# Score products of 64-channel heads on all 128 rows: the lo parts of the keys stored on both halves of the partitions

## The chip, the cores and the metric

The kernel runs on one core of a Trainium2 chip. Its time is the device time of one execution, in microseconds (us); given are the median, the lowest and the highest of three runs. TensorE (PE) computes matrix products, VectorE (DVE) and ScalarE (ACT) elementwise work, GpSimd (POOL) a little of both, and SyncE (SP) issues the transfers.

## What is computed

A network of four layers on 512 tokens of 1024 channels: two hybrid layers (retention, pooling, neighbourhood attention, attention to a memory of 256 tokens, a gated sum of the four, and a feed-forward block), one layer of sliding-window attention beside latent attention, and one layer of dilated attention; the last two are each followed by attention to a memory and by a feed-forward block. What the change touches is the score product of every attention whose heads have 64 channels, here in the words of the reference:

```
scores = jnp.einsum('bhncd,bhnmd->bhncm', qc, kc) * d_intra          # retention
sc = jnp.einsum('bhrnqd,bhrnwkd->bhrnqwk', qg, kg) * (d ** -0.5) + bias   # neighbourhood
sc = jnp.einsum('bhsd,bhmd->bhsm', q, mk) * (q.shape[-1] ** -0.5)    # memory, hybrid layers
s = jnp.einsum('bnqgrd,bnkgd->bngrqk', qb, kk) * (dh ** -0.5)        # window and dilated
```

All of it is in float32, and the sum over d runs over 64 channels of a head.

## The kernel before, in words

**Tiles.** Activations are feature-major: 128 channels on the partitions, 512 tokens along a row. Two heads of 64 channels share a tile, head b=0 on partitions 0 to 63 and head b=1 on 64 to 127.

**Products in three parts.** A float32 value is held as two values of the type fp32r: hi, its rounding, and lo, the rest. The projections (`mm3`, lines 217 to 219; the same three lines in `proj_tok`, 252 to 254) add up hi·hi, lo·hi and hi·lo as three products on 128 rows. Weights come from DRAM in chunks, and ACT (line 209) and DVE (line 210) split each chunk into `wh` and `wl`.

**Scores.** For two heads of 64 the rows of the array hold more than one part at once. `stack_q` (lines 360 to 371) makes for each head b a tile with hi of the queries on the head's own half and lo on the other half. `stack_k` (373 to 395) makes three tiles: for each head its hi keys on both halves (four copies on ACT, line 383 or 385), and one tile `kl` with the lo keys of head 0 on its first half and of head 1 on its second (two subtractions on DVE, line 390 or 392). A score is then two products into one PSUM bank: the stacked queries times hi keys on both halves (128 rows, lines 400 and 714: hi·hi and lo·hi at once), then the hi queries times the lo keys, on the head's own 64 rows alone (lines 401 and 715, "the lo product" below):

```
nc.tensor.matmul(out=out, lhsT=q[b][:, qs], rhs=ks(k[b]), start=True, stop=False)
nc.tensor.matmul(out=out, lhsT=q[b][p, qs], rhs=ks(k[2])[p], start=False, stop=True)
```

In retention the keys are the stationary operand and the queries move (714, 715); elsewhere it is the other way round. In the sliding-window layer no `stack_k` is called: its keys are already the same on both halves, and `ks` holds (hi, hi, lo).

**After the scores.** Softmax (DVE 425 or 427, ACT 429 or 433, DVE 439 and 440), transposes of the probabilities on PE (448) and the product with the values (721, 782, 494, 1029, 471), whose output has 64 columns of the array, one half for each head. Retention multiplies the scores by a decay on DVE (717) instead.

**How often.** `stack_k` is called 20 times: 4 in retention (two head pairs in each of two layers), 4 in neighbourhood attention, 4 for the memory of the hybrid layers, 8 in dilated attention. Score products: 96 pairs in the two hybrid layers, 32 in the sliding window, 64 in dilated attention.

**Order and pools.** The order on each engine is chosen by the framework's scheduler when the program is built. The hybrid layer hands it its steps in the order "R0 R1 Q G N0 N1 B1 F0 F1 B0 M0+M1 B2 B3" (R retention, N neighbourhood, M memory of a head pair; Q and G projections, B gated branches); in dilated attention the projections of the next four heads stand before the attention of the present ones, so that PE has them to do between the scores. Stacked tiles come from the pool `gp` (8 tiles, shared with the gates of the branches), those of the memory keys `mk` from the pool `act` (25 tiles).

Of the kernel before, what the change touches and what calls it, by code (L numbers as in the profile page):

```python
# [9 lines left out]
F32 = mybir.dt.float32  # L10
# [88 lines left out]
class Net:  # L99
# [46 lines left out]
    def gains(self, *which):  # L146
        """Gain vectors as columns: rows of 128 are loaded and transposed on TensorE."""
# [31 lines left out]
    def split(self, src, scale=None, hi=None, lo=None):  # L179
        """hi/lo fp32r pair of src * scale."""  # L180
# [14 lines left out]
    def chunk(self, src, kt, n):  # L195
        """src: list of (dram ap [kt*128 rows, cols], column offset)."""
        nc = self.nc
        with self.tc.high_priority(offset=AHEAD):
            st = self.wp.tile([128, kt, n], F32, name="ws", tag="ws", bufs=2)
            for ap, o in src:  # L200
                w = ap.shape[-1]
                nc.sync.dma_start(out=st[:, :, o:o + w], in_=ap.rearrange("(k p) c -> p k c", p=128))
            return self.chunk_split(st, kt, n)
# [17 lines left out]
    def proj(self, hs, W, c0, ncols, evac, n=512, tags=("acc",)):  # L221
        """Feature-major W[:, c0:c0+ncols]^T @ h; evac(tile index, psum)."""
# [17 lines left out]
    def proj_tok(self, hs, ws, n, toks, evac, tags=("acc",)):  # L240
        """Token-major h^T W for chunks ws (list of (hi, lo, kt)); evac(token tile index, psum [128, n])."""
# [24 lines left out]
    def rsqrt(self, src, w, scale, out=None, last=False):  # L266
        """(src * scale + EPS) ** -0.5 for a small tile."""
# [16 lines left out]
    def norm_stats(self, acc, dim, name, want_bc=True):  # L284
        """acc: [128, 512] sums of squares over channel tiles -> token-major rstd [128, 4] and its broadcast."""
# [15 lines left out]
    def prep(self, k, g, start=False):  # L301
        """Split g * x for the next layer and add up its squares."""
# [18 lines left out]
    def head_stats(self, sq, nt, r):  # L321
        """Squares [128, nt, 64] of nt heads -> r [128, nt], the inverse root mean squares."""
# [4 lines left out]
    def proj_heads(self, hs, W, c0, toks, rt=None):  # L327
        """Token-major projection to four heads of 64, each normed; tiles [128, 2, 256] of two token tiles."""
# [19 lines left out]
    def feature_major(self, tiles, c):  # L348
        """Channels 128 c ... of token-major tiles [128, 2, *] -> PSUM [128, tokens]."""
# [10 lines left out]
    def stack_q(self, src, view=lambda t: t, gp=False):  # L360
        """Two heads of 64 on the partitions of src -> for each head a tile with its hi and its lo part."""
# [11 lines left out]
    def stack_k(self, src, g=None, gp=False, out=None):  # L373
        """Two heads of 64 on the partitions of src -> for each head its hi part twice, and the lo parts of both."""
        nc = self.nc
        out = out or [self.stack_tile(src.shape[-1], gp) for _ in range(3)]
# [9 lines left out]
        kl = out[2]  # L386
        for b in range(2):
            p = slice(64 * b, 64 * b + 64)
            if g is None:
                nc.vector.tensor_tensor(out=kl[p], in0=src[p], in1=out[b][p].bitcast(F32), op=OP.subtract)  # L390
            else:
                nc.vector.scalar_tensor_tensor(out=kl[p], in0=src[p], scalar=g[p], in1=out[b][p].bitcast(F32),
                                               op0=OP.mult, op1=OP.subtract)
        return out

    def scores(self, out, q, k, b, qs, ks):
        """Products of head b of stacked queries (columns qs, on the rows of out) and keys (ks)."""
        nc = self.nc
        p = slice(64 * b, 64 * b + 64)
        nc.tensor.matmul(out=out, lhsT=q[b][:, qs], rhs=ks(k[b]), start=True, stop=False)  # L400
        nc.tensor.matmul(out=out, lhsT=q[b][p, qs], rhs=ks(k[2])[p], start=False, stop=True)  # L401

    def rope(self, ps, C, Sn, out):
        """out = ps * C + halfswap(ps * Sn), heads of 64 on the partitions."""
# [12 lines left out]
    def softmax(self, Sp, n, scale, bias=None, sink=None):  # L417
        """Rows of PSUM scores -> normalized probabilities in SBUF."""
# [24 lines left out]
    def transposes(self, blocks):  # L443
        """blocks: up to four [128, 128] aps -> SBUF tile with their transposes side by side."""
# [9 lines left out]
    def attend_causal(self, heads, scale, bias, O):  # L454
        """Two heads over all queries; heads: (score, vs) with score(out, query block, keys) and vs(j) -> [128, 64]."""
# [18 lines left out]
    def attend_mem(self, heads, scale, O):  # L474
        """One head of 128 or two of 64 against 256 memory keys; heads: (q, k, partitions, vs)."""
# [21 lines left out]
    def load_x(self, x, name, l=0):  # L497
        """x, feature-major, and its split for the first layer."""
# [14 lines left out]
    def mem_norm(self, mem, g):  # L513
        """Feature-major hi/lo of the normed memory: list of 8 ([128, 256] hi, lo)."""
# [28 lines left out]
    def residual(self, hs, W, c0, k0, K, scale, g_next, tags=WIDE):  # L543
        """x += scale * (W^T h); prepares the next norm when g_next is given (False: nothing follows)."""
# [40 lines left out]
    def hybrid(self, l, kv):  # L585
# [16 lines left out]
        # projections  # L602
# [85 lines left out]
        def retention(hp):  # L688
# [18 lines left out]
            for i in range(4):  # L707
                yield
                Ps = []
                for b in range(2):  # L710
                    Sp = self.psum("S")
                    p = slice(64 * b, 64 * b + 64)
                    kc = slice(128 * i, 128 * i + 128)
                    nc.tensor.matmul(out=Sp, lhsT=ks[b][:, kc], rhs=qs[b], start=True, stop=False)
                    nc.tensor.matmul(out=Sp, lhsT=ks[2][p, kc], rhs=qs[b][p], start=False, stop=True)
# [98 lines left out]
        def branch(n, first=False, last=False, tags=WIDE):  # L814
            """Adds the gated branch to the sum over the branches, which takes the place of x until the residual."""
# [39 lines left out]
    def hybrid_kv(self, l):  # L855
        """Keys and values of the memory for a hybrid layer: returns the part for TensorE to be called later."""
        nc, a = self.nc, self.a
        mT = self.mem_norm(a["mem"][0], self.vec("norm_mem_g", 8, l))
        mk = [self.act.tile([128, 2, 256], F32R, name="mk", tag="a") for _ in range(3)]
# [27 lines left out]
    def positions(self):  # L887
        """cos and signed sin tables of the second block from the positions."""
# [58 lines left out]
    def even(self):  # L947
# [11 lines left out]
        # sliding window attention with sinks  # L959
# [3 lines left out]
        def ev_kv(j, ps):  # L963
            if j == 0:
# [3 lines left out]
                for t in k2:  # L968
                    hi, lo = self.split(t)
                    ks.append((hi, hi, lo))  # L970
# [9 lines left out]
        # latent attention: normed ranks  # L980
# [118 lines left out]
    def chunk_rope(self, src, nh):  # L1099
        """Columns in groups of 96 (64 plain, 32 rotary) -> groups of 128 ending in the rotary halves swapped."""  # L1100
# [70 lines left out]
    def rel_bias(self):  # L1171
        """Relative position table in DRAM, one copy per query column, shifted by that column."""
# [18 lines left out]
    def decays(self):  # L1191
        """log sigmoid of the retention decays: lg, nlg [128, 16] (forward layers, then backward layers)."""
# [96 lines left out]
```

## Time and profile before

| what | value |
|---|---|
| time, median of 3 runs | 3154.35 us |
| lowest, highest | 3149.34, 3155.27 us |
| span of the profiled execution (the page gives no other time for it) | 3152.4 us |
| PE busy | 3083.4 us, 98% |
| weight loads busy (PEld, beside PE) | 2500.8 us, 79% |
| DVE busy | 1689.0 us, 54% |
| ACT busy | 1254.3 us, 40% |
| POOL busy | 354.9 us, 11% |
| mean granted clock of PE | 0.984 |

Matrix products overlap: a product's record lasts longer than the time until the next one starts. What a product costs is therefore read from start to start, in the timeline, not from its duration. The shape of a product is written rows*columns of the array, then the moved tile (rows x elements). "Idle" in brackets at a row's end is the time that the engine did nothing before it, and what ended that. A product in full float32 (the values' products) has two records; one in fp32r has one.

### The profile page before, as it was taken

To read this page: it belongs to the slowest core of one execution; us is meant where nothing else is said; L and a number is where in the kernel's file an instruction comes from. 1 tells how busy PE (TensorE), PEld (TensorE's weight loads), DVE (VectorE), ACT (ScalarE), POOL (GpSimd) and SP (SyncE) were. 2 spreads that over 40 slices of the span, in tenths; PEclk is the share of its full clock that TensorE was granted. 3 is DMA by queue.
4 is the path that set the end of the run, shared out by engine and by line. 5 is a ranking of instruction groups with operands and counts; after the bars stand their busy time and mean duration, and the time that the engine had idled before them with its cause. 6 is when DMAs were issued, how large, how long until landed. Compare 5 with 4: busy or idle time off the path is not lost.

```text
span 3152.4 us, 39048 instructions
## 1 busy us (share of the span) xinstructions
PE 3083.4 (98%) x15023; PEld 2500.8 (79%) x15023; DVE 1689.0 (54%) x3054; ACT 1254.3 (40%) x2126; POOL 354.9 (11%) x635
## 2 busy tenths in 40 slices
PE   7989999999999999999999999999999999999998
PEld 6767788888886778888888668788888777888887
DVE  6555555444565564664445775554446666554444
ACT  6443333222463433432223655432225666442222
POOL 2410121000132011120000101010000000010100
PEclk9989999999999999999999899999999999999999
DMA  5312242233342223332322213233332211333332
GB/s 160 108 46 87 73 134 94 96 98 95 126 126 63 70 84 94 124 98 94 100 91 82 52 38 98 74 100 101 94 97 92 66 57 57 94 92 96 100 95 80
DMA packets 288532, 285.62 MB, mean 91 GB/s; under 512 B 23637, under 2 KB 280026, under 8 KB 288346
## 3 DMA queue, kind: packets, MB, share of 16 engines
q1 hardware_dynamic: 288345, 283.13, 29.4%
q8 instruction: 118, 1.93, 0.3%
q14 instruction: 69, 0.56, 0.1%
HBM read 275.37 MB, written 7.71 MB: 90 GB/s over the span
## 4 chain that ended last, share of the span: by engine, by line
PE 95%; DVE 3%; ACT 1%; DMA 1%; issue 1%; POOL 0%; SPq 0%; DVEq 0%; ACTq 0%
PE p_acc L217 11%; PE p_acc L218 11%; PE p_acc L219 11%; PE p_O L217 7%; PE p_O L218 7%; PE p_O L219 7%; PE p_S L218 7%; PE p_S L217 7%; PE p_S L219 7%; PE p_acc L252 2%; PE p_acc L253 2%; PE p_acc L254 2%; PE p_T L448 2%; PE p_S L401 2%; PE p_O L471 1%; PE p_S L400 1%
## 5 line engine op out<-in xcount | busy, mean ns | idle before, releaser
L210 DVE TENSOR_TENSOR wl<-ws,wh 128x1024 fp32r<-128x1024 f32 (+1 forms) x512 | 613.4, 1198 | 751.7 <-ACT wh L209 750.6
L209 ACT CAST wh<-ws 128x1024 fp32r<-128x1024 f32 (+1 forms) x512 | 516.5, 1009 | 1120.2 <-issue 363.1
L217 PE MATMUL p_acc<-hh,wh 128*128 128x512 f32 x1000 | 394.6, 396 | 1.7 <-DVE x L829 1.7
L218 PE MATMUL p_acc<-hh,wl 128*128 128x512 f32 x1000 | 392.5, 393 | 0.0
L219 PE MATMUL p_acc<-hl,wh 128*128 128x512 f32 x1000 | 391.4, 393 | 0.0
L217 PE MATMUL p_O<-hh,wh 128*128 128x512 f32 x680 | 264.4, 390 | 0.3 <-DVE al L188 0.3
L218 PE MATMUL p_O<-hh,wl 128*128 128x512 f32 x680 | 264.5, 390 | 0.0
L219 PE MATMUL p_O<-hl,wh 128*128 128x512 f32 x680 | 264.4, 389 | 0.0
L218 PE MATMUL p_S<-hh,wl 128*128 128x512 f32 x624 | 244.1, 391 | 2.8 <-DVE wl L210 2.8
L217 PE MATMUL p_S<-hh,wh 128*128 128x512 f32 x624 | 243.7, 392 | 2.5 <-ACT wh L209 2.1
L219 PE MATMUL p_S<-hl,wh 128*128 128x512 f32 x624 | 243.7, 391 | 0.0
L571 POOL TENSOR_TENSOR fa<-fa,R_x 128x512 f32<-128x512 f32 x88 | 115.7, 1317 | 1092.6 <-DVE fa L570 1086.2
L217 PEld LDWEIGHTS p_acc<-hh,wh 128*128 128x128 f32 x1000 | 189.0, 189 | 43.9 <-DVE x L829 2.3
L219 PEld LDWEIGHTS p_acc<-hl,wh 128*128 128x128 f32 x1000 | 188.9, 189 | 40.5 <-issue 0.8
L218 PEld LDWEIGHTS p_acc<-hh,wl 128*128 128x128 f32 x1000 | 189.0, 189 | 39.2 <-issue 1.0
L217 PE MATMUL p_acc<-ah,wh 128*128 128x512 f32 x444 | 177.9, 402 | 1.7 <-DVE mlak L1051 1.7
L218 PE MATMUL p_acc<-ah,wl 128*128 128x512 f32 x444 | 174.0, 392 | 0.0
L219 PE MATMUL p_acc<-al,wh 128*128 128x512 f32 x444 | 172.7, 393 | 0.0
L217 PE MATMUL p_S<-ah,wh 128*128 128x512 f32 x392 | 153.3, 392 | 0.3 <-ACT ah L187 0.3
L218 PE MATMUL p_S<-ah,wl 128*128 128x512 f32 x392 | 153.1, 391 | 0.0
L219 PE MATMUL p_S<-al,wh 128*128 128x512 f32 x392 | 151.7, 389 | 0.0
L217 PEld LDWEIGHTS p_O<-hh,wh 128*128 128x128 f32 x680 | 127.5, 188 | 27.2 <-DVE al L188 0.7
(374 smaller groups left out, 5736.0 us busy)
## 6 DMA issues: line engine op xcount, KB each, us to landing
ws<-w_ffn_in SPq DMA_DIRECT2D x88, 512.0 KB
ws<-w_gate SPq DMA_DIRECT2D x64, 512.0 KB
ws<-l_w_gate SPq DMA_DIRECT2D x44, 512.0 KB
ws<-l_w_up SPq DMA_DIRECT2D x44, 512.0 KB
ws<-w_ffn_out SPq DMA_DIRECT2D x40, 512.0 KB
ws<-l_w_down SPq DMA_DIRECT2D x40, 512.0 KB
ws<-w_in SPq DMA_DIRECT2D x36, 512.0 KB
ws<-l_w_qkv SPq DMA_DIRECT2D x24, 512.0 KB
```

The source lines that it names most:

```text
L209: nc.scalar.copy(wh, st)
L210: nc.vector.tensor_tensor(out=wl, in0=st, in1=wh.bitcast(F32), op=OP.subtract)
L217: nc.tensor.matmul(out=out, lhsT=wh[part, k, cols], rhs=hh[part, hn], start=start, stop=False)
L218: nc.tensor.matmul(out=out, lhsT=wl[part, k, cols], rhs=hh[part, hn], start=False, stop=False)
L219: nc.tensor.matmul(out=out, lhsT=wh[part, k, cols], rhs=hl[part, hn], start=False, stop=stop)
L252: nc.tensor.matmul(out=o, lhsT=hh[:, t0:t0 + 128], rhs=wh[:, kk, :], start=k == 0, stop=False)
L253: nc.tensor.matmul(out=o, lhsT=hh[:, t0:t0 + 128], rhs=wl[:, kk, :], start=False, stop=False)
L254: nc.tensor.matmul(out=o, lhsT=hl[:, t0:t0 + 128], rhs=wh[:, kk, :], start=False, stop=k == K - 1)
L400: nc.tensor.matmul(out=out, lhsT=q[b][:, qs], rhs=ks(k[b]), start=True, stop=False)
L401: nc.tensor.matmul(out=out, lhsT=q[b][p, qs], rhs=ks(k[2])[p], start=False, stop=True)
L448: nc.tensor.transpose(pt[:, 128 * i:128 * i + 128], b, self.ident)
L571: nc.gpsimd.tensor_tensor(out=a, in0=a, in1=R, op=OP.mult)
```

## The change

`stack_k` makes four tiles in place of three: the lo keys of head b now lie on both halves of a tile of their own, `out[2 + b]`, which takes four subtractions in place of two. The lo product takes the whole stacked query tile and this tile, so it runs on 128 rows: it adds lo·lo on the other half of the rows, a part that was left out before. The sliding window uses its `lo` tile for both heads, and `mk` has one tile more. Docstrings are gone, so line numbers behind the first ones stay and those after line 711 are one lower (714 and 715 become 713 and 714), while 390 and 392 become 391 and 393.

```diff
     def stack_k(self, src, g=None, gp=False, out=None):
         nc = self.nc
-        out = out or [self.stack_tile(src.shape[-1], gp) for _ in range(3)]
+        out = out or [self.stack_tile(src.shape[-1], gp) for _ in range(4)]
...
-        kl = out[2]
         for b in range(2):
             p = slice(64 * b, 64 * b + 64)
-            if g is None:
-                nc.vector.tensor_tensor(out=kl[p], in0=src[p], in1=out[b][p].bitcast(F32), op=OP.subtract)
-            else:
-                nc.vector.scalar_tensor_tensor(out=kl[p], in0=src[p], scalar=g[p], in1=out[b][p].bitcast(F32),
-                                               op0=OP.mult, op1=OP.subtract)
+            for d in (b, 1 - b):
+                kl = out[2 + b][64 * d:64 * d + 64]
+                if g is None:
+                    nc.vector.tensor_tensor(out=kl, in0=src[p], in1=out[b][p].bitcast(F32), op=OP.subtract)
+                else:
+                    nc.vector.scalar_tensor_tensor(out=kl, in0=src[p], scalar=g[p], in1=out[b][p].bitcast(F32),
+                                                   op0=OP.mult, op1=OP.subtract)
         return out
 
     def scores(self, out, q, k, b, qs, ks):
         nc = self.nc
-        p = slice(64 * b, 64 * b + 64)
         nc.tensor.matmul(out=out, lhsT=q[b][:, qs], rhs=ks(k[b]), start=True, stop=False)
-        nc.tensor.matmul(out=out, lhsT=q[b][p, qs], rhs=ks(k[2])[p], start=False, stop=True)
+        nc.tensor.matmul(out=out, lhsT=q[b][:, qs], rhs=ks(k[2 + b]), start=False, stop=True)
...
                     nc.tensor.matmul(out=Sp, lhsT=ks[b][:, kc], rhs=qs[b], start=True, stop=False)
-                    nc.tensor.matmul(out=Sp, lhsT=ks[2][p, kc], rhs=qs[b][p], start=False, stop=True)
+                    nc.tensor.matmul(out=Sp, lhsT=ks[2 + b][:, kc], rhs=qs[b], start=False, stop=True)
...
-        mk = [self.act.tile([128, 2, 256], F32R, name="mk", tag="a") for _ in range(3)]
+        mk = [self.act.tile([128, 2, 256], F32R, name="mk", tag="a") for _ in range(4)]
...
-                    ks.append((hi, hi, lo))
+                    ks.append((hi, hi, lo, lo))
```

The scheduler answers to it with a slightly different order. Of products there are as many as before. Call it a change of shape where two neighbours on PE differ in whether they use 64 rows, 64 columns or more of both. Before, the order has 602 such places: 187 from a wide product to a lo product, 151 from a lo product to a wide one, 37 from a lo product to a 64-column one, 1 the other way, and 226 between wide and 64-column ones. Now it has 272, all of the last kind. In the two hybrid layers and the sliding window nearly all score products stand where they stood (one moves by 36 products, a few by up to 18); in dilated attention some stand up to 57 products later and some up to 107 earlier.

On PE, the end of the second head pair of retention in the first layer (`p_S<-stack` are score products, `p_O<-RP` products with the values, `p_T` transposes). Before:

```order
L721 MATMUL p_O<-RP,rv_568 64x512
L714 MATMUL p_S<-stack 128x512
L715 MATMUL p_S<-stack 128x512
L721 MATMUL p_O<-RP,rv_568 64x512 x2
L728 MATMUL p_T<-small_cst,retf 128x128 x4
L352 MATMUL p_T<-small_cst,hz 128x128 x8
```

and now:

```order
L720 MATMUL p_O<-RP,rv_569 64x512
L713 MATMUL p_S<-stack 128x512
L714 MATMUL p_S<-stack 128x512
L720 MATMUL p_O<-RP,rv_569 64x512 x2
L727 MATMUL p_T<-small_cst,retf 128x128 x4
L352 MATMUL p_T<-small_cst,hz 128x128 x8
```

Nothing moved here. Such a step had three changes of shape (values to hi, hi to lo, lo to values) and has two now, since hi and lo are both wide.

On PE, the first head pair of retention in the first layer, its first products with the values (two heads, one product each). Before they stood together:

```order
L253 MATMUL p_acc<-wl,hh_109 128x256
L254 MATMUL p_acc<-wh,hl_110 128x256
L721 MATMUL p_O<-RP,rv_567 64x512 x2
L714 MATMUL p_S<-stack 128x512
L252 MATMUL p_acc<-wh,hh_95 128x256
```

Now the first of them stands alone,

```order
L253 MATMUL p_acc<-wl,hh_109 128x256
L254 MATMUL p_acc<-wh,hl_110 128x256
L683 MATMUL p_T<-plo,plw 128x512
L720 MATMUL p_O<-RP,rv_568 64x512
L252 MATMUL p_acc<-wh,hh_95 128x256
```

and the second 37 rows behind it, in front of the next scores:

```order
L253 MATMUL p_acc<-wl,hh_101 128x256
L254 MATMUL p_acc<-wh,hl_102 128x256
L720 MATMUL p_O<-RP,rv_568 64x512
L713 MATMUL p_S<-stack 128x512
L714 MATMUL p_S<-stack 128x512
```

The same happens to one such pair in the second layer, so two heads' products that stood together are apart at two places.

On DVE, the keys of the second head pair of neighbourhood attention in the first layer (`stack<-p_T,hg_na,stack` are the subtractions that make the lo keys, `wl` is the split of weights, `P,sm_m` begins a softmax). Before:

```order
L789 TENSOR_TENSOR al<-p_O,ah 128x512
L392 SCALAR_TENSOR_TENSOR stack<-p_T,hg_na,stack 64x512 x2
L210 TENSOR_TENSOR wl<-ws,wh 128x512
L829 SCALAR_TENSOR_TENSOR x_87<-gate,p_acc 128x512
L425 ISA P,sm_m<-p_S,bm 128x256
```

and now:

```order
L210 TENSOR_TENSOR wl<-ws,wh 128x512
L788 TENSOR_TENSOR al<-p_O,ah 128x512
L393 SCALAR_TENSOR_TENSOR stack<-p_T,hg_na,stack 64x512 x4
L828 SCALAR_TENSOR_TENSOR x_87<-gate,p_acc 128x512
L828 SCALAR_TENSOR_TENSOR x_88<-gate,p_acc 128x512
L425 ISA P,sm_m<-p_S,bm 128x256
```

Four subtractions stand in a row where two stood, and the split of weights that came behind them now comes ahead of them.

## Rows read from the trace of the kernel before

**Rows 1.** The page: busy us of each engine; chain that ended last, by engine.

```profile
PE 3083.4 (98%) x15023; PEld 2500.8 (79%) x15023; DVE 1689.0 (54%) x3054; ACT 1254.3 (40%) x2126; POOL 354.9 (11%) x635
...
PE 95%; DVE 3%; ACT 1%; DMA 1%; issue 1%; POOL 0%; SPq 0%; DVEq 0%; ACTq 0%
```

**Rows 2.** Waits of PE: who waited for whom, us in total, times, longest.

```profile
PE p_S L400 <- ACT stack L385: 6.6, 6, 1.5
```

**Rows 3.** All lo products by shape: duration min/median/max in ns, first and last start.

```profile
L401 PE MATMUL p_S<-stack x96: 378/383/579, 184.7 to 2633.1; 64*128 64x256 f32 x64, 64*128 64x384 f32 x16, 64*128 64x512 f32 x16
L401 PE MATMUL p_S<-mk,stack x32: 377/380/386, 276.6 to 1180.4; 64*128 64x256 f32 x32
L401 PE MATMUL p_S<-al,stack x32: 378/382/579, 1757.8 to 1828.4; 64*128 64x256 f32 x32
L715 PE MATMUL p_S<-stack x32: 491/492/500, 78.7 to 993.8; 64*128 64x512 f32 x32
```

**Rows 4.** Timeline of PE, first retention scores between projections: start, duration, line.

```profile
78.40 0.39 PE L714 MATMUL p_S<-stack 128*128 128x512 f32 x1
78.72 0.49 PE L715 MATMUL p_S<-stack 64*128 64x512 f32 x1
79.14 0.50 PE L714 MATMUL p_S<-stack 128*128 128x512 f32 x1
79.57 0.49 PE L715 MATMUL p_S<-stack 64*128 64x512 f32 x1
79.99 0.39 PE L252 MATMUL p_acc<-wh,mh 128*128 128x256 f32 x1
80.22 0.28 PE L253 MATMUL p_acc<-wl,mh 128*128 128x256 f32 x1
80.34 0.28 PE L254 MATMUL p_acc<-wh,ml 128*128 128x256 f32 x1
```

**Rows 5.** Timeline of PE in a projection: two neighbours of 128 rows, 512 elements.

```profile
279.75 0.40 PE L217 MATMUL p_acc<-hh,wh 128*128 128x512 f32 x1
279.98 0.39 PE L218 MATMUL p_acc<-hh,wl 128*128 128x512 f32 x1
```

**Rows 6.** Timeline of PE: a product of 96 rows behind one of 128.

```profile
1853.22 0.39 PE L219 MATMUL p_acc<-al,wh 128*128 128x512 f32 x1
1853.44 0.38 PE L1076 MATMUL p_S<-mlak,mlaq 96*128 96x128 f32 x2
```

**Rows 7.** Timeline of PE, products with the values: two heads together, one alone.

```profile
119.19 1.08 PE L721 MATMUL p_O<-RP,rv 128*64 128x512 f32 x4
...
130.71 1.07 PE L721 MATMUL p_O<-RP,rv 128*64 128x512 f32 x2
```

**Rows 8.** Timelines of DVE and PE: keys of the second neighbourhood pair.

```profile
221.03 1.53 DVE L392 SCALAR_TENSOR_TENSOR stack<-p_T,hg_na,stack 64x512 fp32r<-64x512 f32 x2 [1.59 <-ACT stack L385]
...
221.83 0.38 PE L401 MATMUL p_S<-stack 64*128 64x256 f32 x1 [0.39 <-DVE stack L392]
222.62 0.58 PE L401 MATMUL p_S<-stack 64*128 64x256 f32 x1 [0.41 <-DVE stack L392]
```

**Rows 9.** Making stacked keys: duration min/median/max in ns, first and last start.

```profile
L385 ACT ACTIVATE stack<-p_T,hg_na x16: 681/683/685, 173.1 to 1049.8; 64x512 fp32r<-64x512 f32 x16
...
L390 DVE TENSOR_TENSOR stack<-dk,stack x16: 664/686/691, 2433.3 to 2622.7; 64x512 fp32r<-64x512 f32 x16
...
L392 DVE SCALAR_TENSOR_TENSOR stack<-p_T,hg_na,stack x8: 741/750/757, 175.9 to 1051.3; 64x512 fp32r<-64x512 f32 x8
```

**Rows 10.** Two stretches: length, busy us of PE, PEld, DVE, ACT, POOL, granted clock.

```profile
1782.00:1830.00 48.00, 43.31 (x196) 27.86 (x194) 35.66 (x151) 26.96 (x87) 4.47 (x9) 0.72 0.09 23
...
2575.00:2635.00 60.00, 57.49 (x359) 40.77 (x359) 43.01 (x161) 41.80 (x102) 0.00 (x0) 0.91 0.09 27
```

**Rows 11.** Timeline of the weight loads beside rows 4.

```profile
78.72 0.18 PEld L715 LDWEIGHTS p_S<-stack 64*128 64x128 f32 x1 [0.24 <-issue]
...
80.10 0.19 PEld L253 LDWEIGHTS p_acc<-wl,mh 128*128 128x128 f32 x1
```

More of the change, by code (lines that the diff above doesn't have):

```diff
@@ L711, in retention @@
                     Sp = self.psum("S")
-                    p = slice(64 * b, 64 * b + 64)
                     kc = slice(128 * i, 128 * i + 128)
                     nc.tensor.matmul(out=Sp, lhsT=ks[b][:, kc], rhs=qs[b], start=True, stop=False)
-                    nc.tensor.matmul(out=Sp, lhsT=ks[2][p, kc], rhs=qs[b][p], start=False, stop=True)
+                    nc.tensor.matmul(out=Sp, lhsT=ks[2 + b][:, kc], rhs=qs[b], start=False, stop=True)
                     P = self.pp.tile([128, 512], F32, name="RP", tag="P")
```

## The prediction

> **What bounds the kernel now.** The page comes first: PE is busy for 98% of the span, and the chain that ended last is PE for 95% [rows 1]. So what PE no longer spends comes off the time, and what DVE or ACT get on top costs nothing as long as PE has something else to do. The list of PE's waits comes next: its longest entry for stacked keys is 6.6 us in 6 waits [rows 2]. That is the gap through which this change could lose.
>
> Then the lo products themselves, grouped by shape: 96, 32, 32 and 32 of them, 192 in all, each on 64 rows [rows 3]. Their durations say nothing, since records overlap; the timeline does. Between projections, the first retention scores start at 78.40, 78.72, 79.14, 79.57, and the next projection's products at 79.99, 80.22 and 80.34 [rows 4]. Two neighbours of 128 rows and 512 elements lie 0.23 apart [rows 5], two of 256 elements 0.12 (80.22 to 80.34). The reader is to see that the products here lie 0.42 apart, although they move the same 512 elements. The excess has two halves. The last product before a change of shape takes 0.09 more (78.40 to 78.72 is 0.32), and the first one behind a change 0.11 more (79.99 to 80.22 is 0.23 for 256 elements); a product that is both takes 0.19 to 0.20 more. From 78.40 to 80.22 are 1.82 us, where four steps of 0.23 and one of 0.12 would be 1.04; four changes of shape (in, out, in, out) lie between: **0.78 / 4 = 0.20 us for one change of shape.** Fewer rows alone don't cost it: a product of 96 rows follows one of 128 and 512 elements after 0.22 [rows 6].
>
> **The change part by part.**
>
> *Changes of shape.* The built order loses 602 - 272 = 330 of them (front matter). 192 lo products have 384 sides; four times two of them are neighbours (8 sides), 38 sides face a 64-column product and stay a change, which leaves 338, and 8 new ones come with the scheduler's moves. 330 x 0.20 = **66.0 us less**. A lo product on 128 rows moves as many elements as before, so beyond that it costs what it did: 0.23 or 0.12.
>
> *Two separated pairs of value products.* Two heads' products of 64 columns run side by side: four records take 1.08 us together, the two records of a single product 1.07 [rows 7]. Two pairs are apart now: 2 x 1.0 = **2.0 us more**.
>
> *The added subtractions.* 20 calls of `stack_k`, two more each: 40, at 0.69 us from SBUF and 0.75 from PSUM [rows 9], on an engine that is busy 54% of the time [rows 1]. Where PE has projections to do, that hides them. It has none at the second neighbourhood pair: DVE begins only when ACT has made its four copies (at 221.03, after 1.59 idle), does two subtractions in 1.53, and each of the two lo products waits for one of them [rows 8]. With four in a row the second lo product waits 2 x 0.75 = 1.5 longer, in each hybrid layer: **3.0 us more**. The split of weights that stood behind them now stands ahead, so nothing else is pushed back there. The last head pair of dilated attention has no projection beside it either: 2 x 0.69 = **1.4 us more**. The other 34 I cost at nothing; without their cover they would be 34 x 0.75 = 25.5 us at most, and that is the upper bound.
>
> *What the softmax takes back.* In two stretches PE is not full: the later part of the sliding window (43.3 of 48 us, DVE at 35.7) and the end of dilated attention (57.5 of 60) [rows 10]. There a faster product partly waits longer for the softmax. The 32 lo products of the sliding window [rows 3] and the 16 of the last two dilated head pairs save 48 x 2 x 0.20 = 19.2 us; I let a sixth of it go, **3 us**, because PE was idle there for 7.2 of 108 us; the bounds are nothing and half (9.6). The granted clock is 0.72 in the first of these stretches, so part of its products run at the lower of the two levels, 1.2 GHz, where a change of shape may cost up to twice as much; a third of its 64 sides, some 20, would give 4 us more.
>
> Sum: 66.0 - 2.0 - 3.0 - 1.4 - 3.0 = 56.6 us less. The profiled span, 3152.4 us, becomes 3095.8; it lies 2.0 below the median of the three runs, and the median becomes 3154.35 - 56.6 = **3097.8, so 3098 us**.
>
> Low end: nothing lost to the softmax, the two exposed stacks free, and the 4 us of the lower clock: 66 - 2 + 4 = 68, 3086; with the price at 0.21 (3.3 more), 3083. High end: all 40 subtractions exposed, which takes 25.5 from the 56.6: 3123.
>
> A rule that speaks against this change, weighed: the 64-row weight load of a lo product begins with its product at 78.72, after 0.24 of idle time, so it was not taken ahead; in the stream of full products the load for the product at 80.22 begins at 80.10 [rows 4, 11], and with 0.23 from start to start against loads of 0.19 nothing of it shows. The Trainium skill, "TensorE: Matmul & The Clock Gate", Part 3 (Packing small matmuls), says that a weight load overlaps products in flight only where their row groups differ. By that rule a lo product on all rows would have to wait for its load, and one on 64 rows would be the one that gains. The trace says the opposite on both counts; the rule's result is the third rival.
>
> **The rivals.**
>
> 1. *The softmax takes back half.* If DVE and ACT, not PE, set the pace of the score stretches wherever two head pairs follow each other, half of the 66 goes: 3154.35 - 33 + 6.4 = 3128. For it: DVE is at 35.7 of 48 in the sliding window [rows 10]. Against: PE is on the chain for 95% [rows 1].
>
> 2. *Slower: keys that come too late.* Place: the 16 stackings of retention, neighbourhood and dilated attention. A head pair now holds 6 of the 8 tiles of the pool `gp` (5 before), so that all four key tiles wait for the scores of the pair before, and then need four copies and, behind them, two (SBUF) to four (PSUM) subtractions: 4 x 0.68 + 4 x 0.75 = 5.7 us four times, 2.7 + 1.4 = 4.1 us twelve times [rows 9], together 72 us. If PE had nothing to do meanwhile, the 66 would be eaten up: 3154.35 - 66 + 2 + 72 = 3162. It decides above 64/72, nine tenths exposed. Against: PE now waits 6.6 us for stacked keys in all [rows 2], and in the new order projections stand between the head pairs as before.
>
> 3. *Exposed weight loads.* 192 x 0.19 = 36 us back (by the row of a load, 0.19 [rows 11]): 3098 + 36 = 3134. It is the rule of the Trainium skill weighed above. Against it stand [rows 4, 5, 11], as said there.
>
> 4. *It does not do what it says.* The 0.20 belong to something else, such as two products in a row into one PSUM bank with a fresh start, and stay: only the costs remain, 2.0 + 3.0 + 1.4: 3154 to 3161. Against: projections also add up in one bank, 0.23 apart, and the first product of the projection behind the lo product is late too [rows 4].
>
> **How the numbers follow.** Forecast 0.83, rivals in order 0.06, 0.04, 0.03, 0.04. The forecast's own range is 3083 to 3123; about 19 in 20 of its cases lie in it, 0.79 of all, so I leave it at that. A difference of 0.2% (6.3 us) is what a measurement of this kernel can tell from none: the three runs spread over 5.9 us. Faster: forecast and rivals 1 and 3, 0.92. Rival 4 is split: same 0.03, slower 0.01. With rival 2, slower 0.05 after rounding up.
>
> **What would show it.** In the profile after: lines 401 and 714 with shape 128*128, hi and lo 0.23 (512) or 0.12 (256) apart between projections; PE's busy time down by some 55 to 60 us at nearly unchanged idle time; 40 more subtractions and up to 30 us more on DVE; line 393 four times in a row and the second lo product behind it 1.5 us later than now; at the start of the first retention pair, single value products of 1.07. Wrong would be: lo products still 0.3 to 0.4 apart (rivals 3, 4), PE's waits for `stack` or for softmax grown by tens of us (2, 1), or a lower granted clock.

## The result, and the profile after

| | before | after |
|---|---|---|
| median of 4 runs (lowest, highest), us | 3152.78 (3149.34, 3155.27) | 3116.60 (3115.65, 3118.37) |
| ratio after to before | | 0.9887, interval 0.9873 to 0.9901 |
| profiled execution: span, us | 3152.4 | 3114.6 (its time 3116.6) |
| mean granted clock | 0.984 | 0.985 |

A fourth run of the kernel before (3151.22) has joined the three, so its median is 3152.78 now. The change gains 36 us. That is faster and inside the range (3083 to 3123), but the sum promised 56.6, and of the span 37.8 are gone. The page after, against [rows 1]:

```profile
PE 3027.0 (97%) x15023; PEld 2487.9 (80%) x15023; DVE 1712.0 (55%) x3094; ACT 1253.5 (40%) x2126; POOL 349.6 (11%) x635
...
PE 93%; DVE 3%; ACT 2%; issue 1%; DMA 1%; SPq 0%; POOL 0%; DVEq 0%; ACTq 0%
```

PE's busy time falls by 56.4 us (3083.4 to 3027.0), but its idle time, span less busy, grows from 69.0 to 87.6. 56.4 - 18.6 = 37.8: a third of what PE no longer does came back as waiting.

That the changes of shape are gone shows at the place of [rows 4], PE's timeline after (start, duration, line):

```profile
79.03 0.40 PE L713 MATMUL p_S<-stack 128*128 128x512 f32 x1
79.26 0.40 PE L714 MATMUL p_S<-stack 128*128 128x512 f32 x1
79.50 0.39 PE L713 MATMUL p_S<-stack 128*128 128x512 f32 x1
79.72 0.40 PE L714 MATMUL p_S<-stack 128*128 128x512 f32 x1
79.96 0.28 PE L252 MATMUL p_acc<-wh,mh 128*128 128x256 f32 x1
80.08 0.28 PE L253 MATMUL p_acc<-wl,mh 128*128 128x256 f32 x1
```

From 79.03 to 80.08 are 1.05 us, where the prediction had 1.82 before and 1.04 without the four changes. The lo products 0.23 apart stand on all 128 rows, as all of them now do; of [rows 3], two lines after:

```profile
L401 PE MATMUL p_S<-stack x96: 278/291/579, 181.0 to 2596.0; 128*128 128x256 f32 x64, 128*128 128x384 f32 x16, 128*128 128x512 f32 x16
...
L714 PE MATMUL p_S<-stack x32: 387/397/398, 79.3 to 977.0; 128*128 128x512 f32 x32
```

Where the rest went is read stage by stage, from the same product to the same product in both traces. Columns as in [rows 10]: start and end, length, busy us of PE, PEld, DVE, ACT, POOL, granted clock. The stages are the memory of the first layer, the sliding window, and dilated attention in three pieces. Inside dilated attention, where the orders differ, the borders stand after the same number of products; a few projection products change sides at the first of them, so the first two pieces are taken together below. Before:

```profile
276.07:345.06 68.99, 68.99 (x327) 54.20 (x327) 39.84 (x78) 26.14 (x53) 10.02 (x7) 1.00 0.27 84
1745.16:1850.01 104.85, 98.99 (x461) 68.87 (x460) 78.49 (x286) 60.22 (x168) 16.48 (x48) 0.82 0.11 27
2425.03:2500.04 75.01, 75.01 (x449) 61.17 (x448) 50.91 (x124) 54.31 (x105) 0.00 (x0) 1.00 0.23 71
2500.04:2577.36 77.32, 77.32 (x456) 59.40 (x454) 50.03 (x143) 55.92 (x115) 0.00 (x0) 1.00 0.20 62
2577.36:2635.17 57.81, 55.30 (x339) 39.32 (x338) 41.56 (x158) 40.69 (x99) 0.00 (x0) 0.91 0.06 20
```

and after:

```profile
270.06:334.34 64.28, 64.28 (x327) 52.66 (x327) 39.57 (x78) 25.90 (x53) 9.33 (x7) 1.00 0.28 86
1719.83:1819.79 99.96, 89.72 (x461) 65.76 (x460) 78.89 (x289) 59.53 (x168) 16.21 (x48) 0.85 0.11 29
2396.00:2466.84 70.84, 70.05 (x449) 61.04 (x449) 51.95 (x125) 51.16 (x100) 0.00 (x0) 1.00 0.25 75
2466.84:2543.36 76.52, 72.78 (x459) 59.84 (x455) 54.24 (x154) 56.55 (x118) 0.00 (x0) 0.96 0.21 63
2543.36:2597.58 54.22, 47.00 (x339) 36.15 (x339) 44.70 (x161) 41.66 (x100) 0.00 (x0) 0.97 0.07 20
```

In the first stage PE is full in both. The changes of shape fall there from 31 to 7, which at 0.20 is 4.8; measured is 68.99 - 64.28 = 4.71. The price holds. The other stages fall short:

| place | changes of shape | at 0.20 us | measured | missing |
|---|---|---|---|---|
| second neighbourhood pair, both layers | 42 to 16 | 5.2 | 0.2 | 5.0 |
| sliding window | 92 to 36 | 11.2 | 4.9 | 6.3 |
| dilated attention, first two pieces | 109 to 41 | 13.6 | 5.0 | 8.6 |
| dilated attention, end | 78 to 35 | 8.6 | 3.6 | 5.0 |
| all else (two separated value pairs 2.0 of it) | 281 to 144 | 27.4 | 24.1 | 3.3 |
| sum | 602 to 272 | 66.0 | 37.8 | 28.2 |

Three places are worth a look. **The second neighbourhood pair**, answering to [rows 8]; PE in the second layer before (the brackets hold the idle time before the row, and what ended it):

```profile
1049.10 0.39 PE L400 MATMUL p_S<-stack 128*128 128x256 f32 x1
...
1053.51 0.79 PE L217 MATMUL p_acc<-hh,wh 128*128 128x512 f32 x1 [0.86 <-DVE x L829]
```

in the second layer after:

```profile
1029.22 0.39 PE L400 MATMUL p_S<-stack 128*128 128x256 f32 x1
1030.62 0.39 PE L400 MATMUL p_S<-stack 128*128 128x256 f32 x1 [1.02 <-ACT stack L385]
1032.16 0.39 PE L401 MATMUL p_S<-stack 128*128 128x256 f32 x1 [1.15 <-DVE stack L393]
1033.72 0.38 PE L401 MATMUL p_S<-stack 128*128 128x256 f32 x1 [1.17 <-DVE stack L393]
1035.16 0.79 PE L217 MATMUL p_acc<-hh,wh 128*128 128x512 f32 x1 [1.06 <-DVE x L828]
```

and in the first layer after, the same stretch:

```profile
214.92 0.39 PE L400 MATMUL p_S<-stack 128*128 128x256 f32 x1 [1.46 <-ACT stack L385]
...
220.14 0.79 PE L217 MATMUL p_acc<-hh,wh 128*128 128x512 f32 x1
```

The two lo products wait 1.15 and 1.17 where they waited 0.39 and 0.41 (in both layers). In the second layer, from the first score to the projection behind are 5.94 us, against 4.41 before (1049.10 to 1053.51): 1.53 more, just as forecast. Products that wait for their keys also gain nothing from the shape, 0.4 for the two changes there; the rest of the 2.4 that are missing lies mostly in the projection products behind. In the first layer the stretch grew by only 0.81 (5.22 against 4.41, 219.65 to 224.06 before), but PE also waits 1.46 us ahead of it for ACT's copies, where the order before had projection products.

**Dilated attention**, middle; PE and DVE after:

```profile
2486.08 0.40 PE L401 MATMUL p_S<-stack 128*128 128x512 f32 x1
2486.21 1.28 DVE L415 TENSOR_TENSOR dq<-rc,ru 128x512 f32<-128x512 f32 x2
...
2487.86 1.37 DVE L391 TENSOR_TENSOR stack<-dk,stack 64x512 fp32r<-64x512 f32 x2
...
2487.91 0.41 PE L448 MATMUL p_T<-small_cst,P 128*128 128x128 f32 x2 [1.43 <-DVE sm_r L439]
...
2489.26 0.69 DVE L412 TENSOR_TENSOR rc<-p_acc,rope 128x512 f32<-128x512 f32 x1
...
2490.01 0.58 PE L252 MATMUL p_acc<-wh,hh 128*128 128x256 f32 x1 [1.69 <-DVE rc L412]
...
2490.39 0.41 PE L253 MATMUL p_acc<-wl,hh 128*128 128x256 f32 x1
2490.60 0.41 PE L254 MATMUL p_acc<-wh,hl 128*128 128x256 f32 x1
```

PE waits 1.69 us for `rc`, the first step by which DVE empties a projection's PSUM bank; the 1.37 us of two subtractions stand directly ahead of it. Behind the wait products of 256 elements lie 0.21 apart instead of 0.12, at a granted clock of 0.50 (2490 to 2492): the lower of the two levels, 1.2 GHz. So here the subtractions delay not the scores for which they work, but what stands behind them on DVE. That accounts for one wait; the one before it, 1.43 for `sm_r` of the softmax, has other work of DVE ahead of it (`dq`, two operations in 1.28). PE is idle for 4.5 of the 8.6 us that are missing in the first two pieces; the other 4.1 are busy time, where the clock is 0.96 in the second piece.

**PE's waits** over the whole run, the entries that answer to [rows 2] or have grown (us in total, times, longest):

```profile
PE p_S L400 <- ACT stack L385: 8.2, 7, 1.5
...
PE p_T L448 <- DVE P L440: 4.7, 5, 2.6
PE p_S L401 <- DVE stack L393: 4.6, 4, 1.2
...
PE p_O L471 <- ACT PT L451: 3.1, 4, 1.6
```

and before, the entry that answers to the third line:

```profile
PE p_S L401 <- DVE stack L392: 1.6, 4, 0.4
```

These waits for keys grew by some 5 us (L400 was 6.6 before [rows 2]), and two small new ones add 2.2 (L400 for the copies of line 383, 1.4; L401 for the subtractions of line 391, 0.8). The others shown are waits for the softmax and what follows it (P, PT).

### The profile page after: what moved, and what is told of

It is laid out like the page before. It is cut to its first block, busy times and chain, and to the rows that moved or that the text cites. A ratio compares the mean times of both kernels' runs of the same rounds, so it can differ in the third digit from the quotient of the medians.

```text
span 3114.6 us, 39083 instructions
## 1 busy us (share of the span) xinstructions
PE 3027.0 (97%) x15023; PEld 2487.9 (80%) x15023; DVE 1712.0 (55%) x3094; ACT 1253.5 (40%) x2126; POOL 349.6 (11%) x635
## 4 chain that ended last, share of the span: by engine, by line
PE 93%; DVE 3%; ACT 2%; issue 1%; DMA 1%; SPq 0%; POOL 0%; DVEq 0%; ACTq 0%
PE p_acc L217 11%; PE p_acc L218 11%; PE p_acc L219 11%; PE p_O L217 7%; PE p_O L219 7%; PE p_O L218 7%; PE p_S L217 7%; PE p_S L218 7%; PE p_S L219 7%; PE p_acc L252 2%; PE p_acc L254 2%; PE p_acc L253 2%; PE p_T L448 2%; PE p_O L471 1%; PE p_O L720 1%; PE p_O L494 1%
```

## The experiments

Two causes could make most of the missing 28 us: the **keys** (a fourth tile: 40 more subtractions, and six of eight pool tiles held), or the **softmax**, which PE now reaches earlier and must wait for. The kernel before, the changed kernel and the experiments each have their own line numbers; every ratio is to the kernel before on the same chip.

**One lo tile for both heads.** The products on 128 rows, without a fourth tile (edit to the changed kernel; line 714 likewise):

```diff
-            for d in (b, 1 - b):
-                kl = out[2 + b][64 * d:64 * d + 64]
+            kl = out[2][p]
...
-        nc.tensor.matmul(out=out, lhsT=q[b][:, qs], rhs=ks(k[2 + b]), start=False, stop=True)
+        nc.tensor.matmul(out=out, lhsT=q[b][:, qs], rhs=ks(k[2]), start=False, stop=True)
```

On the other half of the rows this head's lo queries then meet the other head's lo keys: a small term that the reference does not have.

> The lo product runs on all 128 rows, but over the one tile of lo keys of the kernel before (head 0 on the first half, head 1 on the second): three tiles and two subtractions in each stacking. On the other half of the rows the queries' lo then meets the other head's lo keys, so a term of lo times lo size of the wrong head is added in place of the own head's. The built order has 266 changes of shape (602 before, 272 in the changed kernel), 336 x 0.20 = 67 us less than before. Theory A, the 19 us that the changed kernel lacks against its sum come from making the fourth tile (subtractions on DVE, or the sixth tile in the pool): about 3152.8 - 67 + 3 to 8 of softmax waits = 3089 to 3094 us. Theory B, they come from faster scores that run into the softmax, whatever the keys cost: 3110 to 3119 us, as the changed kernel.

Measured: 3101.50 us, ratio 0.9837 (0.9824 to 0.9851); 266 changes of shape. It lies between the two ranges, 15 us below the changed kernel and 51 below the one before, where its 336 changes fewer would make 67. Both second neighbourhood pairs and the first two pieces of dilated attention now gain in full (missing: -0.6 and 0.6 us in place of 5.0 and 8.6). Sliding window and the end of dilated attention still miss 4.8 and 6.6. So what is missing in the first two places goes with the fourth tile; the last two miss about as much without it.

**The keys alone.** The four tiles of the changed kernel, with the lo product on 64 rows as before:

```diff
-        nc.tensor.matmul(out=out, lhsT=q[b][:, qs], rhs=ks(k[2 + b]), start=False, stop=True)
+        p = slice(64 * b, 64 * b + 64)
+        nc.tensor.matmul(out=out, lhsT=q[b][p, qs], rhs=ks(k[2 + b])[p], start=False, stop=True)
```

> Keys are made as in the changed kernel (four tiles, four subtractions), the lo product runs on the head's own 64 rows as before: the costs of the change without its gain; 605 changes of shape. Theory A: 3152.8 + 2 for two separated value pairs + 3 to 5 for the second neighbourhood pairs + 8 to 12 in dilated attention = 3166 to 3172 us. Theory B: 3152.8 + 2 + 3 = 3155 to 3160 us.

Measured: 3169.05, ratio 1.0054 (1.0040 to 1.0067), 16.5 us slower; 605 changes of shape. The size is as expected, but the trace shows more than waits. Nearly all of it, 15.6 us, lies in dilated attention, and most of that (9.9) at its end:

```profile
2584.80:2652.54 67.74, 64.18 (x339) 45.52 (x339) 45.48 (x161) 42.67 (x101) 0.00 (x0) 0.75 0.05 16
```

Against before's 57.81 us PE is idle for only 1.0 us more (3.56 against 2.51); its busy time grew by 8.9, at a granted clock of 0.75 against 0.91. So the later keys cost little as waits here, and most of the loss goes with the lower clock; that they brought the clock down is not shown by itself. That this 16.5 is close to the 15 between the two versions above is therefore no confirmation of the sum. In the sliding window, where this version has as many changes of shape as the kernel before (92), it is 2.9 us shorter (101.98 against 104.85): stages can differ by that much for reasons that no edit here controls.

**Which part of the keys: DVE's time or the pool?** Two edits to the version with one lo tile: each subtraction done twice, and 7 tiles in `gp` (a head pair holds 5 of them, so two are left, as 6 of 8 leave two).

```diff
+            for _ in range(2):
...
-        self.gp = en(name="gp", bufs=8)
+        self.gp = en(name="gp", bufs=7)
```

> As the run with one lo tile, but each subtraction is done twice into the same place: 40 subtractions more on DVE, five tiles in the pool as before. 272 changes of shape. If within theory A the subtractions make the loss: 3108 to 3116 us, near the changed kernel. If the pool's sixth tile makes it: 3088 to 3096 us, as the run with one lo tile. Theory B: 3110 to 3119 us.

> As the run with one lo tile, but the pool of stacked tiles has 7 in place of 8, so that 2 are free beside a head pair's 5, as 2 are free beside 6 of 8 in the changed kernel; 276 changes of shape (2 us more than with 266), one value pair separated (1 us). If within theory A the pool makes the loss: 3104 to 3114 us. If not: 3 us over the run with one lo tile, 3091 to 3098 us. Theory B: 3110 to 3121 us.

Measured: 3106.97 (0.9855, 0.9842 to 0.9869) and 3105.03 (0.9851, 0.9837 to 0.9864), 5.5 and 3.5 us over the version with one lo tile on the same chip. The first lies in none of its ranges, just under that of the subtractions; the second lies in the pool's. By 0.20 us, 1.2 and 2.0 of this are changes of shape that came back (272 and 276), and the second has a separated value pair again. Neither total makes the 15, but the totals mislead. In the first two pieces of dilated attention the two miss 7.2 and 6.9 us, each nearly the 8.6 of the changed kernel, and both together cannot make it twice: **either is enough** to push the stage out of an order in which PE was full. Over all of dilated attention, one lo tile and then twice the subtractions:

```profile
2386.44:2581.57 195.13, 188.28 (x1240) 156.93 (x1239) 141.44 (x422) 150.84 (x317) 0.00 (x0) 0.97 0.18 58
...
2383.37:2587.73 204.36, 191.18 (x1241) 157.75 (x1239) 150.63 (x438) 150.41 (x317) 0.00 (x0) 0.97 0.17 55
```

Twice the subtractions costs 9.2 us there, the smaller pool 3.6 (198.69), the changed kernel 6.5 (201.58). In the total, 5.5 of the 9.2 are hidden by the sliding window, which neither edit touches and which runs shorter with twice the subtractions (92.46 against 97.99 with one lo tile):

```profile
1716.95:1809.41 92.46, 80.83 (x462) 60.58 (x460) 77.54 (x286) 59.41 (x168) 16.65 (x48) 0.94 0.12 31
```

Here all of 11.2 is gained, though PE is idle for 11.6 us, more than after the change (10.2). The difference to the 99.96 of the changed kernel is in PE's busy time, 80.8 against 89.7, at a clock of 0.94 against 0.85. So it is in all seven versions that have these lo products on 128 rows and the whole softmax (the changed kernel and six of the experiments): PE is idle in this stage for 10.2 to 11.6 us, 4.4 to 5.8 more than before (5.9), and the stage takes 92.5 to 100.0 us, the shorter the higher the granted clock (0.94 to 0.85). Of the 6.3 missing after the change, 4.4 are idle time that came back; the other 1.9 are well within what the clock does to this stage from one version to the next.

**Does the softmax take it back?** Its normalisation left out, in the kernel before and in the version with one lo tile:

```diff
-        r = self.small(1, "sm_r")
-        nc.vector.reciprocal(r, l)
-        nc.vector.tensor_scalar(out=P[:, :n], in0=P[:, :n], scalar1=r, scalar2=None, op0=OP.mult)
```

> The kernel before with a shorter softmax: the reciprocal of the row sums and the multiplication by it (lines 439 and 440) are left out in all attentions, so the probabilities are not normalised. DVE loses 0.16 + 0.35 us and more per softmax. It is the base for the next run; 623 changes of shape in its order (602 before). PE was on the chain for 95%, so little: 3140 to 3156 us under every theory.

> The kernel with one lo tile on 128 rows, with the same shorter softmax (no normalisation); 282 changes of shape, 341 x 0.20 = 68 us less than the run before it. Theory A': what the one-tile kernel lacked against its sum (51 of 67 us came) is taken back by softmax waits; with a shorter softmax more of it comes: 57 to 66 us less than the run before it. Theory B': it is lacking for a reason that has nothing to do with the softmax, such as a price that is smaller than 0.20: 50 to 53 us less.

Measured: 3137.54 (0.9955, 0.9943 to 0.9968) and 3075.97 (0.9761, 0.9747 to 0.9774), on one chip. The first lies below its range. In the kernel before, the shorter softmax alone takes the sliding window from 104.85 to 90.51 us, of which 3.2 are idle time and 11.1 are busy time, at a clock of 0.92 in place of 0.82:

```profile
1742.71:1833.22 90.51, 87.85 (x462) 63.14 (x461) 63.12 (x211) 58.50 (x167) 16.06 (x48) 0.92 0.12 32
```

The difference of the two is 61.6 us, inside the range of Theory A', for 341 changes of shape (623 to 282), which make 68.2: 6.6 missing, where the version with one lo tile misses 16.1 with the whole softmax. The sliding window gains 9.1 of 11.4 (81.39 against 90.51), where one lo tile with the whole softmax gains 6.9 of 11.6. At the end of dilated attention, where that version gains 1.4 of 8.0, the light softmax lets it gain nearly all, 58.82 - 50.35 = 8.5 us of 8.6 (43 changes). Before, light:

```profile
2560.85:2619.67 58.82, 54.82 (x338) 39.41 (x338) 31.25 (x105) 40.97 (x102) 0.00 (x0) 0.91 0.06 20
```

one lo tile, light:

```profile
2510.09:2560.44 50.35, 46.96 (x338) 35.84 (x337) 29.64 (x102) 39.56 (x101) 0.00 (x0) 0.93 0.07 22
```

and one lo tile with the whole softmax:

```profile
2525.19:2581.57 56.38, 49.53 (x338) 38.28 (x337) 41.72 (x158) 41.74 (x101) 0.00 (x0) 0.91 0.07 24
```

With one lo tile, PE is idle there for 6.9 us with the whole softmax (2.5 before) and 3.4 with the light one (4.0 before). The light base is itself 1.0 us longer at this place than the kernel before (58.82 against 57.81), so some of the 8.5 is the base's. By the two differences (16.1 and 6.6) the softmax takes back some 9 us, idle time and clock together.

**Taking the subtractions off DVE**, in the changed kernel, for keys that come from SBUF: the second one of each head on GpSimd, or the second half of the tile filled by a transfer from the first.

```diff
-                    nc.vector.tensor_tensor(out=kl, in0=src[p], in1=out[b][p].bitcast(F32), op=OP.subtract)
+                    (nc.vector if d == b else nc.gpsimd).tensor_tensor(out=kl, in0=src[p], in1=out[b][p].bitcast(F32), op=OP.subtract)
```

```diff
+                    if d == b:
+                        nc.vector.tensor_tensor(out=kl, in0=src[p], in1=out[b][p].bitcast(F32), op=OP.subtract)
+                    else:
+                        nc.sync.dma_start(out=kl.bitcast(F32), in_=out[2 + b][p].bitcast(F32))
```

> The changed kernel, with the second subtraction of each lo tile on POOL in place of DVE where the keys lie in SBUF (retention and dilated attention, 24 of the 40 added ones). If the added subtractions on DVE delay the softmax of dilated attention: some 4 to 7 us under the changed kernel, 3109 to 3113 us. If it is the sixth tile of the pool, or the order alone: no change, 3114 to 3119 us. If POOL is too slow and the scores wait for it: over 3119 us.

> The changed kernel, but where the keys lie in SBUF (retention and dilated attention) the second half of each lo tile is a transfer from its first half in place of a second subtraction: 24 subtractions on DVE fewer than in the changed kernel (as many as before), the pool still holds six tiles of a head pair. If the added subtractions on DVE make the loss in dilated attention: 3108 to 3112 us. If it is that all keys of a head pair must wait for the pair before (the sixth tile): 3114 to 3119 us. If the transfer itself is what the scores wait for: over 3119 us.

Measured: 3115.59 (0.9886, 0.9871 to 0.9901) and 3112.39 (0.9867, 0.9852 to 0.9881). The first says nothing on the question, since DVE was not relieved (duration min/median/max in ns):

```profile
L391 POOL TENSOR_TENSOR stack<-dk,stack x16: 1266/1442/1947, 2399.5 to 2584.1; 64x512 fp32r<-64x512 f32 x16
L391 DVE TENSOR_TENSOR stack<-dk,stack x16: 671/1220/1752, 2400.3 to 2586.3; 64x512 fp32r<-64x512 f32 x16
```

DVE's subtraction got slower beside GpSimd's: its median is 1220 against 686 [rows 9], so half as many take nearly as long; the shortest, 671, had nothing of GpSimd beside it. GpSimd's own time alone was not measured. The second takes 24 subtractions off DVE, lands between its ranges and gains 4 us against the changed kernel, at the edge of what can be told, since the two intervals overlap. 1.2 of it are 6 fewer changes of shape (266). The sliding window, which the edit does not touch, and dilated attention:

```profile
1727.41:1821.18 93.77, 83.42 (x461) 63.08 (x460) 78.25 (x283) 58.97 (x166) 16.34 (x48) 0.91 0.12 30
2397.48:2594.48 197.00, 186.60 (x1241) 154.46 (x1239) 139.33 (x419) 149.01 (x317) 0.00 (x0) 0.99 0.23 68
```

The first is 6.2 us shorter than after the change, at the higher clock. Dilated attention is 4.6 shorter, and its first two pieces miss 4.7 in place of 8.6. Against that, 7.6 us are lost ahead of the sliding window, 3.8 in the retention of each hybrid layer, where PE waits 2.4 for the transfers themselves. So with DVE's subtractions as before and six tiles held, about half of the loss in those two pieces stays; the total says little.

**One lo tile in dilated attention only**, the changed kernel elsewhere:

```diff
-                qs, ks = self.stack_q(q[hp], gp=True), self.stack_k(k[hp], gp=True)
+                qs, ks = self.stack_q(q[hp], gp=True), self.stack_k(k[hp], gp=True, one=True)
```

> The changed kernel, but dilated attention alone has the one lo tile of head 0 and head 1 (its lo products on 128 rows then add lo times lo of the other head, as in the run with one lo tile). By the traces, stage against stage, the changed kernel loses some 7 us to the one-tile kernel in dilated attention and some 9 us in the two hybrid layers and around them. If that holds: 3107 to 3112 us. If the loss lies in the hybrid layers alone: 3115 to 3118 us; in dilated attention alone: 3100 to 3104 us.

Measured: 3106.45, ratio 0.9852 (0.9836 to 0.9869), 10 us below the changed kernel and just under the first range. Of the 15 us that one lo tile everywhere brings, two thirds come with it in this layer alone; by the traces dilated attention gains 8.9 (192.73 against 201.58). Dilated attention in the same three pieces:

```profile
2394.67:2463.70 69.03, 69.03 (x450) 60.25 (x448) 50.32 (x124) 53.68 (x105) 0.00 (x0) 1.00 0.24 73
2463.70:2533.41 69.71, 69.71 (x457) 58.40 (x455) 49.44 (x142) 55.32 (x113) 0.00 (x0) 1.00 0.22 68
2533.41:2587.40 53.99, 48.05 (x339) 37.16 (x337) 41.18 (x158) 41.07 (x101) 0.00 (x0) 0.94 0.09 26
```

In the first two PE is busy for all of their length, and they miss 0.6 us of the sum in place of 8.6. The end misses 4.2 still, about as in the changed kernel (5.0): that part does not go with the fourth tile.

## Why the prediction was right in direction and range, and 19 us off

The range held, but not for the reason that set it. Its high end stood for 25.5 us of exposed subtractions; the 18.8 us that the sum has too much are 8.3 for the softmax, 7.2 for the keys of dilated attention, 2.0 for the neighbourhood pairs and 1.3 for the rest. Of the signs that were named, one failed: PE's busy time fell by 56.4 as said, but its idle time grew by 18.6 instead of staying nearly unchanged.

*The price and the count of changes of shape: right.* Where PE is full, 0.20 us each held (4.71 measured for 4.8; dilated attention with one lo tile 13.6 of 14.2). **Rivals 3 and 4** fall with it: the lo products on all rows start 0.23 behind their neighbour, with their weight loads of 0.19 hidden as [rows 4, 5, 11] had it. The rule that the prediction weighed does not favour 64 rows either, as it read it: the rows of a lo product are among those of the wide product ahead of it. The Trainium skill, "TensorEngine Tiling (Array Packing)", Key Properties, says that a change of tiling mode, not of the tile alone, drains TensorE. The trace agrees that a change costs something: 0.20 us.

*The two separated pairs of value products, 2.0: right.* 0.98 and 1.00 are missing in the two retention stretches.

*The second neighbourhood pairs, 3.0: mis-sized, 5.0.* The delay was right in the second layer (1.53); in the first it was 0.81, beside a new wait of 1.46 for ACT's copies that the sum did not have. The 66 us were also counted at these products: one that waits for its key starts when the key is there, in whatever shape.

*"The other 34 I cost at nothing": the step that failed on the keys.* It priced an added subtraction by whether its own score waits, and the sixth tile of the pool not at all, outside rival 2. In dilated attention most keys come in time; but DVE also empties the projections' PSUM banks, and a projection that is to cover the subtraction can wait for that (1.69 us at the place shown). 8.6 us are missing in the two pieces where I had none (1.4 stood for the last head pair alone). That DVE was busy for only 51 of 75 us in the first of them says nothing about two more operations ahead of the one that PE waits for. One lo tile in this stage brought 8 of the 8.6 back, which shows that the loss goes with the fourth tile; that it is DVE's queue rather than the pool is shown for the one place only, since a smaller pool without any added subtraction lost 6.9 in the same pieces.

*What the softmax takes back, 3: mis-sized, 11.* 6.3 in the sliding window and 5.0 at the end of dilated attention are missing, over even the bound of 9.6. A sixth was too little, and it did not follow from its reason: 7.2 idle of 108 us is a fifteenth. PE's idle share was the wrong measure in any case. Where the softmax sets the pace, about half of the saving came back as waiting: in the sliding window DVE's work stays as it is (78.5 and 78.9 us), and PE's idle time goes from 5.9 to 10.2; at the end of dilated attention it goes from 2.5 to 7.2; together 9.1 of 19.8 us. With the light softmax, the end of dilated attention gained 8.5 us of 8.6, where one lo tile with the whole softmax gained 1.4 of 8.0. What is missing beyond the idle time is busy time, which moves with the clock by more than that from version to version. The 4 us that the low end gave to the lower clock cannot be told apart from this.

*Rival 1* named this mechanism with half of everything taken back (3128). Half is right for these two stages, and for no other. *Rival 2*, keys too late, is what costs the neighbourhood pairs, at 5 us and not 72.

The sum by what was measured: 66.0 - 2.0 - 5.0 - 8.6 - 11.3 - 1.3 (rest) = 37.8.

What stays open: how the 8.6 us of dilated attention divide between DVE's time and the sixth pool tile. Each edit alone cost about 7 us there, six tiles without the added subtractions left 4.7, and the scheduler answers each with another order. A larger pool was not tried, and neither was the changed kernel in the order of the version with one lo tile.

**The faster version** is the one lo tile for both heads: 3101.5 us, ratio 0.9837, against 0.9887 for the change; the intervals do not overlap. It adds a term of lo times lo that belongs to the other head, except in the sliding window.

## What to carry to other kernels

Between wide products, a product on half the rows costs two changes of shape, 0.4 us here, more than the 0.23 that the product itself takes; filling the other rows was cheaper here, even with something small and unwanted. Look for a filling that needs no new work: whatever the engine beside PE does for it is paid where PE waits for that engine, and not only where its own result is late. Price a saving on PE stage by stage: where the softmax sets the pace, about half of it came back here as idle time. And read an experiment by stages too: a stage that the edit does not touch differed by up to 7.5 us between versions, along with its granted clock.

## What the runs showed of the hardware that was not expected

A subtraction on DVE takes longer beside one on GpSimd, both reading SBUF: 686 ns on DVE alone, 1220 beside GpSimd's 1442 (medians). The Trainium skill, "SBUF — State Buffer", section "SBUF: two separate sides", says that these two engines share a pair of ports, held by one instruction at a time. The slower rows of DVE agree with that; moving work from the one to the other brought nothing here.

What PE takes for the same products can outweigh the waits between them. In the middle of dilated attention products lay 0.21 apart instead of 0.12 behind the waits of 1.43 and 1.69 us shown above. In the kernel with the keys alone, 1.0 us more of idle time at the end of dilated attention stands beside 8.9 us more of busy time, at a granted clock of 0.75 against 0.91. But the sum of the idle time does not decide it: the sliding window took PE 80.8 us at 0.94 with 11.6 us of idle time, and 89.7 at 0.85 with 10.2. Which waits bring the clock down was not singled out.
